# Splitting weights 2048 columns at a time, and moving the tokens' sums, in a float32 two-layer decoder trunk

## The chip, the cores and the metric

The kernel runs on one core of a Trainium2 chip. The metric is the device time of one execution in microseconds (us). Five engines work side by side and meet at semaphores: PE multiplies matrices, DVE and ACT do elementwise work, SP issues the DMAs that bring weights in, POOL is hardly used. Each engine takes its own instructions strictly in the order in which they stand in its queue, except that PE loads weights ahead.

## The reference

All arithmetic is float32. Cut to what matters here:

```python
D_MODEL = 2048; SEQ = 256; DEPTH = 2; N_Q_HEADS = 12; N_KV_HEADS = 4; N_MEM_HEADS = 4; D_FF = 4 * D_MODEL

for layer in range(DEPTH):
    # 12 query heads in 4 groups, each group with one K and V head; layer 0 has sinks and a window
    proj = h @ w_in[layer]                  # q, k, v and the memory heads' queries
    self_out = attention(q, k, v)
    mem_out = memory_attention(qm, mem, w_mem_kv[layer])
    mix = concatenate([self_out, mem_out]) @ w_o[layer]
    h = layer_norm(ALPHA * h + mix, ...)
    ffn = square(relu(h @ w_up[layer])) @ w_down[layer]
    h = layer_norm(ALPHA * h + ffn, ...)
return h
```

## The kernel before

**Products.** PE has no full float32 product at full rate, so every weight and activation is split in two parts, `hi` (a cast on ACT) and `lo` (the rest, a subtraction on DVE): `split`, lines 95 to 97. A product is then three matmuls, hi by hi, lo by hi and hi by lo. Every weight of the model passes through this split once, streamed from memory in tiles of 2048 columns (1 MB) by SP.

**Buffers.** A raw tile sits in one of `NRAW = 4` slots. Its split parts go to buffers `whi` and `wlo` of 1024 columns, `NHI = 7` of each, so a tile needs two of each. A buffer comes free when PE has done its last matmul with it; the cast that fills it next waits for that.

**The program's stages, per layer.** First the projections of the attention: `wform` computes K or Q of one head from one weight tile, 16 steps of k. When its last step is done, `wform_sum` adds the two halves of the result (`sb` on ACT at line 197, then `kt` or `qt` on DVE at line 198). Per group there is one K and three Q. The heads' attention runs in stages hooked into the projections that follow: at step k = 10 of the next projection PE computes a head's scores (lines 343 and 344, from `qt` and `kt`), at k = 14 it transposes an earlier head's weights, at k = 4 it multiplies by V. Then come the memory heads' queries (scores at line 370), the output projection (`aform`), a layer norm (`normed`), and the MLP.

**The MLP.** It works in chunks of 2048 hidden columns, four per layer: two "up" groups (`v_` = 0 and 1), which make the hidden activations, and two "down" groups, which use them. Each is an `mlp_group` of eight weight tiles ("units", K = 256 each) in the order `ORDER`. Units 0 and 1 are "fast": they stand third and fifth and use seven block products in place of eight, with sums of weight blocks (`t`, lines 116 to 120) and sums of activation blocks (`fast_acts`). The sums of the layer's input (`sum_h`) are made once per layer, before its first such group. The sums of a chunk's hidden activations (`sum_g`) are made from `gt[0]`. What an up group has made is transposed in hooks of the group after it (`UHOOKS`: in its first and second unit, lines 426 to 429), and `sum_g` is made in the third of these hooks of the up group with `v_` = 1.

**What sets the order.** The source calls the operations in the order of the loops, and a scheduler that builds the program reorders each engine's queue by its own estimates. So a cast for a later weight tile can stand ahead of a small operation that PE waits for, or behind it.

Of the kernel before, what the change touches and what calls it, by code (L numbers as in the profile page):

```python
# [8 lines left out]
F32 = mybir.dt.float32  # L9
# [6 lines left out]
P = 128  # L16
# [15 lines left out]
SLOPES = [2.0 ** (-8.0 * (i + 1) / HEADS) for i in range(HEADS)]  # L32
FAR = -1e33
NRAW = 4
NHI = 7
NLG = 4
HOLD = 13
HOLDF = 14
# [26 lines left out]
WHOOKS = (10, 14, 4)  # L65
NWARM = 2
FILL = (10, 11, 12, 16)
ORDER = (2, 3, 0, 4, 1, 5, 6, 7)
FAST = (0, 1)
UHOOKS = ((0, 3), (1, 0), (1, 2), (1, 3))  # L70
WTAIL = ((1, 2), (2, 0), (3, 1), (5, 2), (7, 1), (9, 2))

# [2 lines left out]
def trunk(ctx: ExitStack, tc: tile.TileContext, a: dict, out: bass.AP):  # L75
# [23 lines left out]
    def fast_weights(src):  # L99

        raw = wp.tile([P, 2048], F32, name="raw", tag="raw", bufs=NRAW)
        nc.sync.dma_start(raw, src)
        b = raw.rearrange("p (q c) -> p q c", q=4)
        t_ = wp.tile([P, 4, 512], F32, name="t", tag="raw", bufs=NRAW)
        tiles = []

        def pair(s, n):
            hi = wp.tile([P, 1024], F32R, name="whi", tag="whi", bufs=NHI)  # L110
            lo = wp.tile([P, 1024], F32R, name="wlo", tag="wlo", bufs=NHI)
            split(hi[:, :n], lo[:, :n], s)
            tiles.extend([(hi[:, c:c + 512], lo[:, c:c + 512]) for c in range(0, n, 512)])

        pair(raw[:, :1024], 1024)
        nc.vector.tensor_tensor(t_[:, 0:2], b[:, 0:2], b[:, 2:3].broadcast_to([P, 2, 512]), ALU.subtract)
        pair(b[:, 3], 512)
        pair(t_[:, 0:2].rearrange("p q c -> p (q c)"), 1024)
        nc.vector.tensor_tensor(t_[:, 2], b[:, 1], t_[:, 0], ALU.add)
        nc.vector.tensor_tensor(t_[:, 3], b[:, 3], t_[:, 2], ALU.subtract)  # L120
        pair(t_[:, 2:4].rearrange("p q c -> p (q c)"), 1024)
        return dict(zip(("B11", "B22", "B21", "T1", "T3", "T2", "T4"), tiles))

    def fast_acts(x, s_):


        raw = wp.tile([P, 2048], F32, name="x_f", tag="raw", bufs=NRAW)
        f = raw[:, :1024].rearrange("p (k t) -> p k t", k=4)
        nc.vector.tensor_tensor(f, x[:, :, 0].bitcast(F32), x[:, :, 1].bitcast(F32), ALU.add)
        a11, a21 = f[:, 0:4:2, :P], f[:, 0:4:2, P:]  # L130
        a12, a22 = f[:, 1:4:2, :P], f[:, 1:4:2, P:]
        s = raw[:, 1024:].rearrange("p (q u t) -> p q u t", q=4, u=2)
        nc.vector.scalar_tensor_tensor(s[:, 0], a21, -1.0, a22, op0=ALU.mult, op1=ALU.subtract)
        nc.vector.scalar_tensor_tensor(s[:, 1], s[:, 0], -1.0, a11, op0=ALU.mult, op1=ALU.subtract)
        nc.vector.tensor_tensor(s[:, 2], a11, a21, ALU.subtract)
        nc.vector.tensor_tensor(s[:, 3], a12, s[:, 1], ALU.subtract)
        split(s_[:, 0], s_[:, 1], raw[:, 1024:])

    def weights(src, parts=1):


        raw = wp.tile([P, 2048], F32, name="raw", tag="raw", bufs=NRAW)
        n = 2048 // parts
        for c in range(0, 2048, n):
            nc.sync.dma_start(raw[:, c:c + n], src[:, c:c + n])
        halves = []
        n = min(n, 1024)
        for s in range(2):
            hi = wp.tile([P, 1024], F32R, name="whi", tag="whi", bufs=NHI)
            lo = wp.tile([P, 1024], F32R, name="wlo", tag="wlo", bufs=NHI)  # L150
            for c in range(0, 1024, n):
                split(hi[:, c:c + n], lo[:, c:c + n], raw[:, s * 1024 + c:s * 1024 + c + n])
            halves.append((hi, lo))
        return halves

    def new_acts(tag, nm):
        return [ap_.tile([P, 4, 2, T], F32R, name=f"{nm}{j}", tag=f"{tag}{j}") for j in range(KT // 4)]
# [74 lines left out]

        return ps, finish

    def mlp_group(src, xts, sums, hooks, early):

        ps = [ps_mm.tile([P, 512], F32, name="ps_g", tag="mm") for _ in range(4)]
        own = {}  # L240
        seen = {}
        last = {}
        plan = []
        for u in ORDER:
            plan.extend([(u, b) for b in range(4)] if u not in FAST else [(u, i) for i in range(7)])

        fast = ("P1", 0, 1, "P5", "P7", "P6", 2)
        for u in ORDER:
            for i in range(7 if u in FAST else 4):
                last[fast[i] if u in FAST else i] = (u, i)  # L250

        def mm3(bank, x, w, st, en):
            (xh, xl), (hi, lo) = x, w
            nc.tensor.matmul(bank, xh, hi, start=st, stop=False)  # L254
            nc.tensor.matmul(bank, xh, lo, start=False, stop=False)  # L255
            nc.tensor.matmul(bank, xl, hi, start=False, stop=en)  # L256

        def tok(k, t):
            return [xts[k // 4][:, k % 4, s, t * P:(t + 1) * P] for s in range(2)]

        left = len([u for u in ORDER if u in FAST])
        for pos, u in enumerate(ORDER):
            k0, k1 = 2 * u, 2 * u + 1
            if u in FAST:
                for i in range(4):
                    hooks.get((pos, i), nothing)()
                if not own:
                    for nm in ("P1", "P5", "P6", "P7"):
                        own[nm] = ps_at.tile([P, 512], F32, name=nm, tag="at")
                w = fast_weights(src[u])  # L270
                sx = [[sums[:, s, q, u % 2] for s in range(2)] for q in range(4)]
                prods = (("P1", tok(k0, 0), "B11"), (0, tok(k1, 0), "B21"), (1, sx[3], "B22"),
                         ("P5", sx[0], "T1"), ("P7", sx[2], "T3"), ("P6", sx[1], "T2"), (2, tok(k1, 1), "T4"))
                for i, (b, x, wn) in enumerate(prods):
                    mm3(own[b] if b in own else ps[b], x, w[wn], b not in seen, last[b] == (u, i))
                    seen[b] = True
                left -= 1
                if not left:
                    early(own)
                continue  # L280
            (h0, l0), (h1, l1) = weights(src[u])
            w = {"B11": (h0[:, :512], l0[:, :512]), "B22": (h0[:, 512:], l0[:, 512:]),
                 "B12": (h1[:, :512], l1[:, :512]), "B21": (h1[:, 512:], l1[:, 512:])}
            for b in range(4):
                hooks.get((pos, b), nothing)()
                t, n = b // 2, b % 2 + 1
                mm3(ps[b], tok(k0, t), w[f"B1{n}"], b not in seen, False)
                mm3(ps[b], tok(k1, t), w[f"B2{n}"], False, last[b] == (u, b))
                seen[b] = True
        return ps  # L290
# [289 lines left out]
    for l in range(LAYERS):  # L580
# [34 lines left out]
        for c in range(FF // CH):  # L615
            gt = new_acts("og", "gT")
            todo = []
            sum_g = ap_.tile([P, 2, 4, 2, P], F32R, name="sum_g", tag="sum_g")
            for v_ in range(CH // 1024):

                hooks = dict(zip(UHOOKS, todo))
                us = [None] * 4
                if c == 0 and v_ == 0 and not more:
                    for nb in range(2):
                        ps, fin = aform([a["wup_s"][nb, i] for i in range(4)], hT, hold=(16 if nb == 0 else 0))
                        if nb == 0:
                            us[0] = relu2(ps[0])
                            fin()
                            us[2] = relu2(ps[1])
                        else:  # L630
                            us[1], us[3] = relu2(ps[0]), relu2(ps[1])
                else:
                    if sum_h is None:
                        sum_h = ap_.tile([P, 2, 4, 2, P], F32R, name="sum_h", tag="sum_h")
                        fast_acts(hT[0], sum_h)
                    acc = []
                    ps = mlp_group(a["wup"][l, c * (CH // 1024) + v_], hT, sum_h, hooks, sums_up(acc))
                    for b in range(4):
                        nc.vector.tensor_tensor(acc[b], acc[b], ps[b], ALU.add)
                        nc.scalar.activation(acc[b], acc[b], AF.Relu)  # L640
                        nc.scalar.activation(acc[b], acc[b], AF.Square)
                    us = acc

                def back(b, v_=v_, us=us, gt=gt, sum_g=sum_g):
                    transposed(us[b], gt[2 * v_ + b % 2], b // 2, 0)
                    if v_ == 0 and b == 2:
                        fast_acts(gt[0], sum_g)
                todo = [lambda b=b, f=back: f(b) for b in (0, 1, 2, 3)]
            last = c == FF // CH - 1
            if last and more:  # L650
# [1 line left out]
            for v_ in range(D // 1024):  # L652
                if last and v_ == 1:
                    for nb in range(2, 4):
                        ps, fin = aform([a["wdn_s"][l, nb - 2, i] for i in range(4)], gt,
                                        hold=(0 if nb == 2 else 8 if more else HOLDF))
                        if nb == 2:
                            for t in range(NT):
                                residual(h, ps, t, nb, False, st)
                    continue  # L660
                ps = mlp_group(a["wdn"][l, v_, 8 * c:8 * c + 8], gt, sum_g, dict(zip(UHOOKS, todo)),
                               sums_down(h, v_, c == 0))
                todo = []
                for b in range(4):
                    residual(h, {b // 2: ps[b]}, b // 2, 2 * v_ + b % 2, False, st if last else None)
# [63 lines left out]
```

## Time and profile before

| | us |
|---|---|
| median of 3 runs | 2082.78 (2081.52 to 2083.8) |
| profiled execution, own time | 2085.73 |
| its span, first to last instruction | 2083.6 |
| PE busy | 2023.7 (97%) |
| DVE busy | 1540.2 (74%) |
| ACT busy | 1045.6 (50%) |
| mean granted TensorE clock | 0.984 of 2.4 GHz |

The span is what the views measure. The execution's own time is 2.1 us longer, and 2.95 us above the median of the runs. An engine's idle time costs time only where PE, which is busy for nearly all of the span, waits for it.

### The profile page before, as it was taken

The numbers are of one execution on the slowest core, as the hardware profiler recorded it, in microseconds if no ns is written. First come the engines' busy times: TensorE is split into PE (matmuls) and PEld (weight loads), VectorE is DVE, ScalarE is ACT, GpSimd is POOL, SyncE is SP. The second block draws the span as 40 slices with busy tenths as digits, with TensorE's granted clock in tenths as the row PEclk, the third lists the DMA queues.
The fourth block names the chain that finished last, engine by engine and source line by source line (L and its number), as shares of the span: only waits on it lengthen the run. The fifth ranks groups of instructions, "written<-read, shape, count | busy, mean of one in ns | idle before, by whom it ended". The sixth has DMA issues, their size and how long they took to land.

```text
span 2083.6 us, 23980 instructions
## 1 busy us (share of the span) xinstructions
PE 2023.7 (97%) x9326; PEld 1675.4 (80%) x9326; DVE 1540.2 (74%) x1951; ACT 1045.6 (50%) x1351; POOL 1.2 (0%) x8
## 2 busy tenths in 40 slices
PE   9999999999999999999999999999999999999997
PEld 7888888788778878878888888778887887888786
DVE  6566669688597868768885665769786876877785
ACT  5555535554464455456444554346445544654551
POOL 0000000000000000000000000000000000000000
PEclk9999999999999999999999999999999999999999
DMA  9644545455356545445754445425654554564562
GB/s 330 255 143 160 202 162 203 160 204 181 142 208 220 197 157 205 175 146 219 271 222 171 153 162 202 142 103 211 221 194 161 203 177 146 214 219 173 205 220 81
DMA packets 56273, 391.63 MB, mean 188 GB/s; under 512 B 6368, under 2 KB 6368, under 8 KB 9696
## 3 DMA queue, kind: packets, MB, share of 16 engines
q1 hardware_dynamic: 56160, 390.10, 52.1%
q8 instruction: 73, 1.20, 0.2%
q14 instruction: 40, 0.33, 0.0%
HBM read 387.98 MB, written 2.10 MB: 187 GB/s over the span
## 4 chain that ended last, share of the span: by engine, by line
PE 92%; DVE 6%; ACT 1%; issue 0%; DMA 0%; SPq 0%; DVEq 0%; ACTq 0%
PE ps_g L256 17%; PE ps_g L255 17%; PE ps_g L254 17%; PE ps_w L189 7%; PE ps_a L211 5%; PE ps_a L212 5%; PE ps_a L213 5%; PE ps_w L191 4%; PE P L254 3%; PE P L256 3%; PE P L255 3%; PE pt_h L426 2%; PE ps_m L536 1%; PE ps_m L538 1%; PE ps_m L537 1%; DVE h L419 1%
## 5 line engine op out<-in xcount | busy, mean ns | idle before, releaser
L97 DVE TENSOR_TENSOR wlo<-raw,whi 128x1024 fp32r<-128x1024 f32 (+1 forms) x706 | 815.7, 1174 | 329.0 <-ACT whi L96 324.9
L96 ACT CAST whi<-raw 128x1024 fp32r<-128x1024 f32 (+1 forms) x706 | 693.5, 1014 | 596.3 <-PE ps_g L256 323.6
L255 PE MATMUL ps_g<-wlo,hT 128*128 128x512 f32 x780 | 305.8, 392 | 0.1
L256 PE MATMUL ps_g<-whi,hT 128*128 128x512 f32 x780 | 305.9, 392 | 0.0
L254 PE MATMUL ps_g<-whi,hT 128*128 128x512 f32 x780 | 302.6, 395 | 0.9 <-ACT whi L96 0.7
L254 PE MATMUL ps_g<-whi,gT 128*128 128x512 f32 x728 | 285.3, 393 | 0.0
L256 PE MATMUL ps_g<-whi,gT 128*128 128x512 f32 x728 | 283.5, 390 | 0.0
L255 PE MATMUL ps_g<-wlo,gT 128*128 128x512 f32 x728 | 283.4, 390 | 0.0
L96 ACT CAST whi<-t 128x1024 fp32r<-128x1024 f32 x116 | 122.0, 1052 | 120.9 <-PE ps_g L256 45.0
L254 PEld LDWEIGHTS ps_g<-whi,hT 128*128 128x128 f32 x780 | 147.8, 190 | 33.7 <-ACT whi L96 3.8
L255 PEld LDWEIGHTS ps_g<-wlo,hT 128*128 128x128 f32 x780 | 147.7, 189 | 31.3 <-DVE wlo L97 0.5
L256 PEld LDWEIGHTS ps_g<-whi,hT 128*128 128x128 f32 x780 | 147.6, 189 | 31.0
L97 DVE TENSOR_TENSOR wlo<-t,whi 128x1024 fp32r<-128x1024 f32 x116 | 141.6, 1223 | 41.2 <-ACT whi L96 40.9
L256 PEld LDWEIGHTS ps_g<-whi,gT 128*128 128x128 f32 x728 | 136.7, 188 | 28.8
L255 PEld LDWEIGHTS ps_g<-wlo,gT 128*128 128x128 f32 x728 | 136.8, 188 | 27.6
L254 PEld LDWEIGHTS ps_g<-whi,gT 128*128 128x128 f32 x728 | 136.6, 188 | 27.2
L189 PE MATMUL ps_w<-hT,whi 128*128 128x512 f32 x320 | 119.9, 414 | 0.0
L189 PE MATMUL ps_w<-xT,whi 128*128 128x512 f32 x320 | 119.9, 414 | 0.0
L211 PE MATMUL ps_a<-whi,ot 128*128 128x512 f32 x256 | 101.7, 397 | 0.0
L213 PE MATMUL ps_a<-whi,ot 128*128 128x512 f32 x256 | 99.8, 390 | 0.0
L212 PE MATMUL ps_a<-wlo,ot 128*128 128x512 f32 x256 | 99.7, 389 | 0.0
L429 DVE TENSOR_TENSOR gT<-pt_h,gT 128x512 fp32r<-128x512 f32 x64 | 43.9, 688 | 67.0 <-ACT gT L428 67.0
(184 smaller groups left out, 2910.1 us busy)
## 6 DMA issues: line engine op xcount, KB each, us to landing
raw<-in_wup_dram SPq DMA_DIRECT2D x120, 1024.0 KB, 4.9
raw<-in_wdn_dram SPq DMA_DIRECT2D x112, 1024.0 KB, 4.9
raw<-in_wo_dram SPq DMA_DIRECT2D x32, 1024.0 KB, 4.8
raw<-in_wq_dram SPq DMA_DIRECT2D x24, 1024.0 KB, 4.8
raw<-in_wdn_s_dram SPq DMA_DIRECT2D x16, 1024.0 KB, 4.9
raw<-in_wmk_dram SPq DMA_DIRECT2D x8, 1024.0 KB, 6.2
raw<-in_wv_dram SPq DMA_DIRECT2D x8, 1024.0 KB, 7.3
raw<-in_wk_dram SPq DMA_DIRECT2D x8, 1024.0 KB, 4.8
```

The lines of the kernel that those rows point to most:

```text
L96: nc.scalar.copy(hi, src)
L97: nc.vector.tensor_tensor(lo, src, hi.bitcast(F32), ALU.subtract)
L189: nc.tensor.matmul(ps, hi[:, kk:kk + P], x.rearrange("p s t -> p (s t)"), start=(k == 0), stop=False)
L191: nc.tensor.matmul(ps[:, :T], lo[:, kk:kk + P], x[:, 0], start=False, stop=(k == KT - 1))
L211: nc.tensor.matmul(ps[t], xh, hi, start=st, stop=False)
L212: nc.tensor.matmul(ps[t], xh, lo, start=False, stop=False)
L213: nc.tensor.matmul(ps[t], xl, hi, start=False, stop=en)
L254: nc.tensor.matmul(bank, xh, hi, start=st, stop=False)
L255: nc.tensor.matmul(bank, xh, lo, start=False, stop=False)
L256: nc.tensor.matmul(bank, xl, hi, start=False, stop=en)
L426: nc.tensor.transpose(pt[:, k], src[:, k * P:(k + 1) * P], ident)
L429: nc.vector.tensor_tensor(xt[:, :, 1, t * P:(t + 1) * P], pt, hi.bitcast(F32), ALU.subtract)
```

## The change

The split buffers become 2048 columns wide, four of each: 8192 columns in place of 7168. A weight tile is split by one cast and one subtraction. In a fast unit the first 1536 columns (B11, B22, B21) are split at once, then all four sums of weight blocks are made, and all 2048 of their columns are split at once; the order of the blocks in memory is changed so that these 1536 are adjacent. The sums of the tokens (activation blocks) become a generator in two steps: `sum_h` is made in hooks of the first and second unit of the first group that uses it, `sum_g` in hooks at the sixth and seventh unit of the up group with `v_` = 1. Their buffers share tags with `v` and `mk`, and are split 512 columns at a time. `UP` and `DOWN` hold the same order and the same two fast units as before, so PE's products are the same.

```diff
-NHI = 7
+NHI = 4
...
-ORDER = (2, 3, 0, 4, 1, 5, 6, 7)
-FAST = (0, 1)
+UP = ((2, 3, 0, 4, 1, 5, 6, 7), 2)
+DOWN = ((2, 3, 0, 4, 1, 5, 6, 7), 2)
...
-        def pair(s, n):
-            hi = wp.tile([P, 1024], F32R, name="whi", tag="whi", bufs=NHI)
-            lo = wp.tile([P, 1024], F32R, name="wlo", tag="wlo", bufs=NHI)
+        def pairs(s, n):
+            hi = wp.tile([P, 2048], F32R, name="whi", tag="whi", bufs=NHI)
+            lo = wp.tile([P, 2048], F32R, name="wlo", tag="wlo", bufs=NHI)
             split(hi[:, :n], lo[:, :n], s)
...
-        pair(raw[:, :1024], 1024)
-        nc.vector.tensor_tensor(t_[:, 0:2], b[:, 0:2], b[:, 2:3].broadcast_to([P, 2, 512]), ALU.subtract)
-        pair(b[:, 3], 512)
-        pair(t_[:, 0:2].rearrange("p q c -> p (q c)"), 1024)
+        pairs(raw[:, :1536], 1536)
+        nc.vector.tensor_tensor(t_[:, 0:2], b[:, 0:2], b[:, 3:4].broadcast_to([P, 2, 512]), ALU.subtract)
         nc.vector.tensor_tensor(t_[:, 2], b[:, 1], t_[:, 0], ALU.add)
-        nc.vector.tensor_tensor(t_[:, 3], b[:, 3], t_[:, 2], ALU.subtract)
-        pair(t_[:, 2:4].rearrange("p q c -> p (q c)"), 1024)
+        nc.vector.tensor_tensor(t_[:, 3], b[:, 2], t_[:, 2], ALU.subtract)
+        pairs(t_.rearrange("p q c -> p (q c)"), 2048)
...
-    def fast_acts(x, s_):
+    def fast_acts(xs, units):
+        parts = []
+        for j in range(0, len(units), 2):
...
+            parts += [s[:, u] for u in range(n)]
+        yield
+        for (hi, lo), s in zip(units, parts):
+            split(hi, lo, s)
+        yield
...
     def weights(src, parts=1):
-        halves = []
-        n = min(n, 1024)
-        for s in range(2):
-            hi = wp.tile([P, 1024], F32R, name="whi", tag="whi", bufs=NHI)
-            lo = wp.tile([P, 1024], F32R, name="wlo", tag="wlo", bufs=NHI)
-            for c in range(0, 1024, n):
-                split(hi[:, c:c + n], lo[:, c:c + n], raw[:, s * 1024 + c:s * 1024 + c + n])
+        hi = wp.tile([P, 2048], F32R, name="whi", tag="whi", bufs=NHI)
+        lo = wp.tile([P, 2048], F32R, name="wlo", tag="wlo", bufs=NHI)
+        for c in range(0, 2048, n):
+            split(hi[:, c:c + n], lo[:, c:c + n], raw[:, c:c + n])
+        return [(hi[:, c:c + 1024], lo[:, c:c + 1024]) for c in (0, 1024)]
...
-                        sum_h = ap_.tile([P, 2, 4, 2, P], F32R, name="sum_h", tag="sum_h")
-                        fast_acts(hT[0], sum_h)
+                        sum_h = sum_units(UP[1], ("sum_h0", "sum_h1", "pts"))
+                        steps = fast_acts(hT, sum_h)
+                        hooks[0, 0] = hooks[1, 1] = lambda s=steps: next(s)
+                    if v_ == 1:
+                        steps = fast_acts(gt, sum_g)
+                        hooks[5, 0] = hooks[6, 0] = lambda s=steps: next(s)
...
-                    if v_ == 0 and b == 2:
-                        fast_acts(gt[0], sum_g)
```

The first place is ACT's queue in the first up group with `v_` = 1 of layer 0. The names `gT0` and `gT1` are the transposed hidden activations of the group before; `whi_3297` (before) and the casts after it are the first fast unit's weights. Before:

```order
L428 CAST gT1_2850<-pt_h_3237 128x4x128
L428 CAST gT0_2849<-pt_h_3256 128x4x128
L428 CAST gT1_2850<-pt_h_3277 128x4x128
L96 CAST sum_g_2853<-x_f_3263 128x1024
L96 CAST whi_3297<-raw_3294 128x1024
L96 CAST whi_3302<-raw_3294 128x512
L96 CAST whi_3306<-t_3296 128x1024
```

And now, where `whi_3050` holds the first fast unit's sums of weight blocks (its `raw` part is cast further up), `whi_3108` and `whi_3115` are the second fast unit's, and `whi_3151` is the unit's after that:

```order
L97 CAST whi_3050<-t_3042 128x2048
L439 CAST gT0_2647<-pt_h_2972 128x4x128
L97 CAST whi_3077<-raw_3075 128x2048
L439 CAST gT1_2648<-pt_h_2991 128x4x128
L439 CAST gT0_2647<-pt_h_3010 128x4x128
L439 CAST gT1_2648<-pt_h_3023 128x4x128
L97 CAST whi_3108<-raw_3105 128x1536
L97 CAST whi_3115<-t_3107 128x2048
L97 CAST whi_3151<-raw_3149 128x2048
L97 CAST sums_2651<-x_f_3155 128x512
L97 CAST sums_2652<-x_f_3155 128x512
```

All of the first fast unit's casts now stand ahead of the transposes' casts, and the tokens' sums behind those of the second.

The second place is DVE's queue in the attention of layer 0, at the end of a group's last Q projection. `lg`, `mx`, `nm`, `den` and `rec` are an earlier head's softmax; `qt_1309` (before) and `qt_1223` (now) are the query that PE needs for the scores. Before:

```order
L346 SCALAR_TENSOR_TENSOR lg_1344<-dist_a_399,ps_s_1341 128x384
L351 TENSOR_REDUCE mx_1346<-lg_1344 128x1 x2
L354 TENSOR_SCALAR nm_1349<-mx_1346,nsink_411 128x2
L364 TENSOR_TENSOR den_1351<-den_1351,es_1354 128x2
L316 RECIPROCAL rec_1357<-den_1351 128x2
L198 TENSOR_TENSOR qt_1309<-ps_w_1320,sb_1379 128x256
```

And now:

```order
L357 SCALAR_TENSOR_TENSOR lg_1254<-dist_a_373,ps_s_1251 128x384
L362 TENSOR_REDUCE mx_1256<-lg_1254 128x1 x2
L365 TENSOR_SCALAR nm_1259<-mx_1256,nsink_385 128x2
L98 TENSOR_TENSOR wlo_1492<-raw_1489,whi_1491 128x2048
L375 TENSOR_TENSOR den_1261<-den_1261,es_1264 128x2
L212 TENSOR_TENSOR qt_1223<-ps_w_1230,sb_1289 128x256
```

A 2048-column subtraction now stands ahead of `den` and the query.

## Rows read from the trace of the kernel before

**Rows 1.** The page, busy time of each engine, share of the span, instructions

```profile
PE 2023.7 (97%) x9326; PEld 1675.4 (80%) x9326; DVE 1540.2 (74%) x1951; ACT 1045.6 (50%) x1351; POOL 1.2 (0%) x8
```

**Rows 2.** Waits of PE: total us, times, longest

```profile
PE P L254 <- ACT whi L96: 38.3, 16, 3.5
```

**Rows 3.** Windows: stretch, length, busy by engine, granted clock, DMA share, GB/s

```profile
513.42:608.03 94.61, 89.81 (x390) 73.14 (x388) 68.39 (x76) 49.69 (x60) 0.00 (x0) 0.96 0.49 178
608.03:694.24 86.21, 86.21 (x389) 71.41 (x388) 73.49 (x83) 44.31 (x51) 0.00 (x0) 1.00 0.55 196
1388.54:1440.97 52.43, 47.56 (x204) 38.11 (x202) 40.09 (x46) 26.93 (x34) 0.00 (x0) 0.93 0.48 175
```

**Rows 4.** Timeline, ACT and PE, third unit of an up group: start, length, instruction

```profile
389.19 1.04 ACT L96 CAST sum_g<-x_f 128x1024 fp32r<-128x1024 f32 x1 [2.24 <-DVE x_f L136]
390.14 1.56 ACT L96 CAST whi<-raw 128x1024 fp32r<-128x1024 f32 x2
...
391.24 0.50 PE L254 MATMUL P<-whi,hT 128*128 128x512 f32 x1 [3.51 <-ACT whi L96]
...
393.76 0.80 PE L254 MATMUL P<-whi,sum_h 128*128 128x512 f32 x1 [1.27 <-ACT whi L96]
```

**Rows 5.** Timeline, the same place in the down group that follows

```profile
429.68 1.04 ACT L96 CAST whi<-t 128x1024 fp32r<-128x1024 f32 x1
...
439.98 0.39 PE L254 MATMUL P<-whi,gT 128*128 128x512 f32 x1
```

**Rows 6.** Groups by shape, DVE and ACT: busy, mean ns, idle before

```profile
L97 DVE TENSOR_TENSOR wlo<-raw,whi 128x1024 fp32r<-128x1024 f32 x644 | 776.0, 1221 | 326.9 <-ACT whi L96 322.8
L97 DVE TENSOR_TENSOR wlo<-raw,whi 128x512 fp32r<-128x512 f32 x62 | 42.3, 686 | 2.0 <-ACT whi L96 2.0
...
L96 ACT CAST whi<-raw 128x1024 fp32r<-128x1024 f32 x644 | 657.1, 1052 | 552.4 <-PE ps_g L256 282.4 <-PE ps_a L213 156.2 <-PE ps_w L189 63.0
...
L96 ACT CAST whi<-raw 128x512 fp32r<-128x512 f32 x62 | 38.4, 620 | 43.9 <-PE ps_g L256 41.2 <-DMA raw<-in_wmv_dram 2.1
```

**Rows 7.** Timeline of the attention, a group's second Q, then its third

```profile
149.72 1.05 ACT L96 CAST whi<-raw 128x1024 fp32r<-128x1024 f32 x1 [2.44 <-PE ps_w L189]
...
151.95 0.15 DVE L364 TENSOR_TENSOR den<-den,es 128x2 f32<-128x2 f32 x1
...
152.22 0.40 DVE L198 TENSOR_TENSOR qt<-ps_w,sb 128x256 f32<-128x256 f32 x1
...
153.17 0.38 PE L343 MATMUL ps_s<-kt,qt 128*128 128x128 f32 x2
...
155.91 0.39 PE L189 MATMUL ps_w<-xT,whi 128*128 128x512 f32 x1
...
160.46 0.38 PE L343 MATMUL ps_s<-kt,qt 128*128 128x128 f32 x2
```

**Rows 8.** Timeline, the next group's first Q, then a memory head's query

```profile
170.28 1.05 ACT L96 CAST whi<-raw 128x1024 fp32r<-128x1024 f32 x1
...
172.50 0.42 DVE L198 TENSOR_TENSOR qt<-ps_w,sb 128x256 f32<-128x256 f32 x1
...
174.36 0.38 PE L343 MATMUL ps_s<-kt,qt 128*128 128x128 f32 x2
...
213.97 1.05 ACT L96 CAST whi<-raw 128x1024 fp32r<-128x1024 f32 x1
...
217.53 1.02 PE L370 MATMUL ps_m<-mk,qt 128*128 128x256 f32 x4
```

**Rows 9.** Timeline of PE and windows, layer norm of layer 1's attention

```profile
1336.58 1.32 PE L426 MATMUL pt_h<-ident,h 128*128 128x128 f32 x8 [2.04 <-DVE h L420]
...
1351.87 1.29 PE L426 MATMUL pt_h<-ident,h 128*128 128x128 f32 x8 [1.64 <-DVE h L420]
...
1338.10:1341.50 3.40, 3.40 (x11) 2.75 (x11) 3.23 (x6) 1.01 (x2) 0.00 (x0) 0.50 0.60 246
1349.00:1353.00 4.00, 2.33 (x14) 1.53 (x12) 3.86 (x10) 0.47 (x1) 0.00 (x0) 1.00 0.17 70
```

More of the change, by code (lines that the diff above doesn't have):

```diff
@@ L122, in fast_weights @@
+        pairs(t_.rearrange("p q c -> p (q c)"), 2048)
         return dict(zip(("B11", "B22", "B21", "T1", "T3", "T2", "T4"), tiles))
-    def fast_acts(x, s_):
[L127 to L137, printed above, removed]
+    def fast_acts(xs, units):
+        parts = []
+        for j in range(0, len(units), 2):
+            n = len(units[j:j + 2])
+            x = xs[j // 2][:, :2 * n]
+            raw = wp.tile([P, 2, 8, P], F32, name="x_f", tag="raw", bufs=NRAW)
+            f = raw[:, 0, :4 * n].rearrange("p (k t) c -> p k (t c)", t=2)
+            nc.vector.tensor_tensor(f, x[:, :, 0].bitcast(F32), x[:, :, 1].bitcast(F32), ALU.add)
+            a11, a21 = f[:, 0:2 * n:2, :P], f[:, 0:2 * n:2, P:]
+            a12, a22 = f[:, 1:2 * n:2, :P], f[:, 1:2 * n:2, P:]
+            s = raw[:, 1, :4 * n].rearrange("p (u q) c -> p u q c", q=4)
+            nc.vector.scalar_tensor_tensor(s[:, :, 0], a21, -1.0, a22, op0=ALU.mult, op1=ALU.subtract)
+            nc.vector.scalar_tensor_tensor(s[:, :, 1], s[:, :, 0], -1.0, a11, op0=ALU.mult, op1=ALU.subtract)
+            nc.vector.tensor_tensor(s[:, :, 2], a11, a21, ALU.subtract)
+            nc.vector.tensor_tensor(s[:, :, 3], a12, s[:, :, 1], ALU.subtract)
+            parts += [s[:, u] for u in range(n)]
[3 more added lines that the diff above has]
+        yield
@@ L139, in weights, with sum_units @@
+    def sum_units(n, tags):
+        units = []
+        for tag in tags[:n]:
+            if tag == "pts":
+                units.append([ap_.tile([P, 4, P], F32R, name="sums", tag="pts", bufs=2) for _ in range(2)])
+            else:
+                t_ = ap_.tile([P, 2, 4, P], F32R, name="sums", tag=tag)
+                units.append([t_[:, s] for s in range(2)])
+        return units
     def weights(src, parts=1):
@@ L145, in weights @@
             nc.sync.dma_start(raw[:, c:c + n], src[:, c:c + n])
-        halves = []
-        n = min(n, 1024)
-        for s in range(2):
-            hi = wp.tile([P, 1024], F32R, name="whi", tag="whi", bufs=NHI)
-            lo = wp.tile([P, 1024], F32R, name="wlo", tag="wlo", bufs=NHI)
-            for c in range(0, 1024, n):
-                split(hi[:, c:c + n], lo[:, c:c + n], raw[:, s * 1024 + c:s * 1024 + c + n])
-            halves.append((hi, lo))
-        return halves
+        hi = wp.tile([P, 2048], F32R, name="whi", tag="whi", bufs=NHI)
[3 more added lines that the diff above has]
+        return [(hi[:, c:c + 1024], lo[:, c:c + 1024]) for c in (0, 1024)]
     def new_acts(tag, nm):
@@ L233, in aform, with mlp_group @@
         return ps, finish
-    def mlp_group(src, xts, sums, hooks, early):
+    def mlp_group(src, xts, sums, hooks, early, order, nfast):
         ps = [ps_mm.tile([P, 512], F32, name="ps_g", tag="mm") for _ in range(4)]
@@ L242, in mlp_group @@
         last = {}
-        plan = []
-        for u in ORDER:
-            plan.extend([(u, b) for b in range(4)] if u not in FAST else [(u, i) for i in range(7)])
         fast = ("P1", 0, 1, "P5", "P7", "P6", 2)
-        for u in ORDER:
-            for i in range(7 if u in FAST else 4):
-                last[fast[i] if u in FAST else i] = (u, i)
+        for u in order:
+            for i in range(7 if u < nfast else 4):
+                last[fast[i] if u < nfast else i] = (u, i)
         def mm3(bank, x, w, st, en):
@@ L259, in tok @@
             return [xts[k // 4][:, k % 4, s, t * P:(t + 1) * P] for s in range(2)]
-        left = len([u for u in ORDER if u in FAST])
-        for pos, u in enumerate(ORDER):
+        left = nfast
+        for pos, u in enumerate(order):
             k0, k1 = 2 * u, 2 * u + 1
-            if u in FAST:
+            if u < nfast:
                 for i in range(4):
@@ L270, in mlp_group @@
                 w = fast_weights(src[u])
-                sx = [[sums[:, s, q, u % 2] for s in range(2)] for q in range(4)]
+                sx = [[s[:, q] for s in sums[u]] for q in range(4)]
                 prods = (("P1", tok(k0, 0), "B11"), (0, tok(k1, 0), "B21"), (1, sx[3], "B22"),
@@ L282, in mlp_group @@
             w = {"B11": (h0[:, :512], l0[:, :512]), "B22": (h0[:, 512:], l0[:, 512:]),
-                 "B12": (h1[:, :512], l1[:, :512]), "B21": (h1[:, 512:], l1[:, 512:])}
+                 "B21": (h1[:, :512], l1[:, :512]), "B12": (h1[:, 512:], l1[:, 512:])}
             for b in range(4):
@@ L617, in trunk @@
             todo = []
-            sum_g = ap_.tile([P, 2, 4, 2, P], F32R, name="sum_g", tag="sum_g")
+            sum_g = sum_units(DOWN[1], ("v", "mk"))
             for v_ in range(CH // 1024):
@@ L633, in trunk @@
                     if sum_h is None:
-                        sum_h = ap_.tile([P, 2, 4, 2, P], F32R, name="sum_h", tag="sum_h")
-                        fast_acts(hT[0], sum_h)
+                        sum_h = sum_units(UP[1], ("sum_h0", "sum_h1", "pts"))
[4 more added lines that the diff above has]
+                        hooks[5, 0] = hooks[6, 0] = lambda s=steps: next(s)
                     acc = []
-                    ps = mlp_group(a["wup"][l, c * (CH // 1024) + v_], hT, sum_h, hooks, sums_up(acc))
+                    ps = mlp_group(a["wup"][l, c * (CH // 1024) + v_], hT, sum_h, hooks, sums_up(acc), *UP)
                     for b in range(4):
@@ L642, in trunk, with back @@
                     us = acc
-                def back(b, v_=v_, us=us, gt=gt, sum_g=sum_g):
+                def back(b, v_=v_, us=us, gt=gt):
                     transposed(us[b], gt[2 * v_ + b % 2], b // 2, 0)
-                    if v_ == 0 and b == 2:
-                        fast_acts(gt[0], sum_g)
                 todo = [lambda b=b, f=back: f(b) for b in (0, 1, 2, 3)]
@@ L661, in trunk @@
                 ps = mlp_group(a["wdn"][l, v_, 8 * c:8 * c + 8], gt, sum_g, dict(zip(UHOOKS, todo)),
-                               sums_down(h, v_, c == 0))
+                               sums_down(h, v_, c == 0), *DOWN)
                 todo = []
@@ L696, in quads @@
         b = w.reshape(k // 256, 2, P, n // 1024, 2, 512).transpose(3, 0, 2, 1, 4, 5)
-        return np.ascontiguousarray(np.stack([b[:, :, :, 0, 0], b[:, :, :, 1, 1], b[:, :, :, 0, 1], b[:, :, :, 1, 0]],
+        return np.ascontiguousarray(np.stack([b[:, :, :, 0, 0], b[:, :, :, 1, 1], b[:, :, :, 1, 0], b[:, :, :, 0, 1]],
                                              axis=3)).reshape(n // 1024, k // 256, P, 2048)
```

## The prediction

> **What bounds the kernel now.** I read the engines' busy times first: PE is busy for 97% of the span, DVE for 74%, ACT for 50% [rows 1]. So PE sets the time, and only what makes PE wait, or lowers its clock, can be won or lost. PE's matmuls are the same in number and kind in both kernels.
>
> Next I read the waits of PE. One line carries nearly all: 38.3 us in 16 waits of the first fast product for its weights' cast on ACT [rows 2]. The windows place them. A pair of up groups and a pair of down groups have the same work on PE (388 weight loads each), yet the up pair takes 94.61 us and the down pair 86.21, and the granted clock is 0.96 in the one and 1.00 in the other [rows 3]. The timeline of one such place shows the cause: ACT must cast `sum_g`, which waits for DVE's sums, before it casts the weights of the first fast unit. PE idles for 3.51 us and again for 1.27 us, and its matmuls then run at half rate for a while (a step of 0.43 us where 0.23 is usual), so the clock has fallen to the lower of its two levels, 1.2 GHz [rows 4]. In the down group the hooks transpose in the same way, but nothing of `sum_g` is made, and the sums of weights have been cast 10 us before PE's first fast product begins, without a wait [rows 5].
>
> **The change part by part.**
>
> *The tokens' sums move.* In the new order ACT casts all of the first fast unit's weights before the transposes' casts, as the down group does now, and `sum_g` after those of the second fast unit. Each up group with `v_` = 1 then costs what its PE work costs. There are eight: seven stand in whole pairs, each worth 94.61 - 86.21 = 8.4 us; the eighth, in layer 1's first chunk, stands alone and takes 52.43 us [rows 3], against half of a down pair with one more set of transposes, 43.1 + 0.7 = 43.8 us, so 8.6 us. Together 7 x 8.4 + 8.6 = 67.4 us. The half-clock stretch is inside this, since the windows contain it. What is late next in these groups? DVE has 68.4 us of work in an up pair [rows 3]; in 86.2 us that leaves it 17.8 us idle. I went through the first three units with these durations. The first fast product's weights are split before the group begins, the sums of weight blocks about 8 us into it, and PE needs them about 14 us into it. The sums of the tokens, 4 us on DVE, fall beside the fifth and sixth unit, whose weights have a lead of some 6 us; they are needed only in the next group. So I cost the moved step at nothing; if that cover were gone, it would cost its length, 4 us a place.
>
> *Wider splits.* A cast of 1024 columns takes 1.05 us and of 512 columns 0.62, so by a straight line 2048 take 1.05 + 2 x 0.43 = 1.92 us. A subtraction takes 1.22 and 0.69 us, so 2048 take 2.29 us [rows 6]. The work is the same. One tile now costs one instruction where it cost two, but neither engine is the bound, so what is saved per instruction is worth nothing.
>
> What the width costs is delay for whoever stands behind it. In the attention a query reaches PE by a short chain after its projection's end: `sb` on ACT, `qt` on DVE, then the scores on PE, ten steps into the next projection. In the new order a 2048-column cast, which waits for the buffer that this same projection's end frees, stands ahead of `sb`; and its 2048-column subtraction stands ahead of `qt`. Before, each was half as long, or stood behind. Behind the subtraction wait `den`, the query, and with the query PE itself. For the group's second Q: the buffer is free and the cast starts at 149.72, and `qt` is done at 149.72 + 1.92 + 2.29 + 0.15 (`den`) + 0.40 = 154.48; PE wants it at 153.17 [rows 7]. That is a wait of 1.3 us. For the third Q the last matmul with the buffer ends at 155.91 + 0.39 = 156.30, the query is ready at 156.30 + 4.76 = 161.06, and PE wants it at 160.46: 0.6 us [rows 7]. For the first Q no `den` stands there: 170.28 + 4.61 = 174.89 against 174.36, so 0.5 us [rows 8]. K is needed later than one projection, and waits for nothing. Per group of four projections that is 2.4 us, in eight groups 19.2 us. Among the memory heads three queries stand behind such a subtraction; the one I worked out is ready at 213.97 + 4.76 = 218.73 and wanted at 217.53 [rows 8], so 1.2 us, and three make 3.6 us. The attention loses about 22.8 us.
>
> No row shows these waits, so I bound them. Below: nothing, if the casts start earlier than the buffers let me think. Above: all 27 of them at the full lengthening of both instructions, 0.87 + 1.07 = 1.94 us, without the slack that the rows show: 52 us. I take 22.8, since it comes from the very places.
>
> The Trainium skill has a rule that speaks against this part ("Perfetto Trace Analysis", "Optimizing Scalar/DVE Operations"): where ScalarE and VectorE are not saturated but cause bubbles elsewhere, break instructions up. By that rule the attention pays, as I reckon it does. The same section prices a grouped instruction at some 60 ns saved on VectorE and 93 ns on ScalarE; by that alone the sum would have the attention's 22.8 us at nothing. The busy shares above are those of engines that are not saturated, so the first half of the rule is the one that applies.
>
> *The rest.* The layer norms, the start and the output projections get the same work in other pieces. The first group of layer 0 now has its first tile split before the norm ends; the norm in layer 1 has a residual moved ahead of PE's transposes, but one more quarter of a tile to hide behind. I cost these at nothing together, with 4 us to each side, the size of the two waits of 2.04 and 1.64 us that stand in layer 1's norm [rows 9].
>
> *Sum.* The profiled execution took 2085.73 us, with a span of 2083.6. 2085.73 - 67.4 + 22.8 = 2041.1 us. It stands 2.95 us above the median of the runs shown, 2082.78, so I predict a median of 2038 us.
>
> **The rivals.**
>
> *The attention doesn't wait.* For it: PE has no wait anywhere in the attention now, and four tiles of lead are more than three and a half. Against it: the buffer that the cast waits for is freed by the projection's own end, so lead doesn't help. It would give 2082.78 - 67.4 = 2015 us.
>
> *PE still waits in the MLP.* The first fast unit's sums are now split as one piece, only after all four are made, and its buffer comes free only when the group before has ended. If half of the 67.4 us stayed, the time would be 2038 + 34 = 2072 us. Against it: the 6 us of lead that I count above, and the down groups, which run free with nearly that order.
>
> *The short waits lower the clock (slower than before).* After a wait of 2.04 us, with light transposes, PE's clock stood at 0.50 for 3.4 us; after one of 1.64 us it stayed at 1.00 [rows 9]. If the new waits in the attention, 0.5 to 1.3 us each, had the effect of the longer one, each of the 27 would cost 3.4 x 0.5 = 1.7 us more, 46 us in all: 2038 + 46 = 2084, level with before. If they had the effect of those in the MLP, where the rate stays low for about 6.8 us, it would be 27 x 3.4 = 92 us: 2130 us. The change is slower from the point at which these waits cost more than 67.4 us, 2.5 us each.
>
> The Trainium skill ("TensorE: Matmul & The Clock Gate", Part 1) says that the throttled state is the default and that activity releases it; by it many small gaps could cool PE. The trace agrees for a long gap and not for the 1.64 us one.
>
> **How the numbers follow.** The forecast 0.62, no wait in the attention 0.18, half of the MLP's waits staying 0.10, the clock 0.06, something that I do not see, either way, 0.04. For 8 in 10: the forecast's own bounds are 2085.73 - 2.95 - 67.4 = 2015 with no wait in the attention and 2067 with all 52 us, or 4 us beyond with the norms. I take 2012 to 2062, which holds the first rival and most of the forecast's upper half, and leaves out the other two. Two kernels of this length can be told apart from about 0.2%, 4 us. Faster: the forecast, the first two rivals and half of the unseen, 0.92, less a little for a bad mixture, 0.90. Slower: half of the clock's and of the unseen, 0.06. The same: 0.04.
>
> **What would show it.** In the profile after: PE's waits for `whi` in the first fast product gone, up pairs and down pairs within 1 us of each other and a clock of 1.00 in both. In the attention, new waits of PE at the scores for `qt`, three in each four projections, of about 1.3, 0.6 and 0.5 us. The forecast is wrong if up pairs still take over 90 us, if the scores wait for nothing, or if the clock falls in the attention.

## The result, and the profile after

The changed kernel takes a median of 2019.42 us (2017.79 to 2019.5), against 2082.6 us before on the same chip: a ratio of 0.9695, 95% interval 0.9678 to 0.9711. I had forecast 2038 us, in a range of 2012 to 2062. The direction was right and the time lies in the range, but the gain is 63 us where I forecast 45. One term of the sum was wrong by 20 us.

The busy times of the engines, from the page of the changed kernel:

```profile
PE 1996.1 (99%) x9326; PEld 1659.4 (82%) x9326; DVE 1505.6 (75%) x1554; ACT 992.7 (49%) x954; POOL 1.2 (0%) x8
```

PE runs the same 9326 matmuls as before [rows 1] and is now busy for 99% of a span of 2016.0 us. The waits of PE are what is left of its idle time:

```profile
PE pt_h L437 <- DVE h L431: 3.2, 1, 3.2
PE ps_m L547 <- ACT whi L97: 1.7, 2, 1.5
PE ps_warm L94 <- DVE warm L91: 1.5, 1, 1.5
...
```

The line of the first fast product, 38.3 us in 16 waits [rows 2], is gone, and no other line of that size has come. The windows of the same three stretches as in [rows 3] (length, busy of PE, PEld, DVE, ACT, POOL, granted clock, DMA share, GB/s):

```profile
504.19:590.45 86.26, 86.26 (x390) 71.41 (x389) 69.90 (x61) 47.27 (x40) 0.00 (x0) 1.00 0.55 195
590.45:676.66 86.21, 86.21 (x390) 71.42 (x388) 68.74 (x59) 42.07 (x31) 0.00 (x0) 1.00 0.54 195
1354.55:1398.61 44.06, 44.06 (x204) 36.50 (x203) 37.52 (x37) 24.59 (x23) 0.00 (x0) 1.00 0.53 191
```

A pair of up groups now takes 86.26 us at a clock of 1.00, like a pair of down groups. It took 94.61 at 0.96. The place of [rows 4] in the timelines of ACT and PE:

```profile
376.40 1.90 ACT L97 CAST whi<-t 128x2048 fp32r<-128x2048 f32 x1
378.61 0.59 ACT L439 CAST gT<-pt_h 128x512 fp32r<-128x512 f32 x1 [0.31 <-PE pt_h L437]
...
386.65 0.39 PE L265 MATMUL P<-whi,hT 128*128 128x512 f32 x1
```

The sums of weight blocks are cast at 376.40, ahead of the transposes' casts and 10 us before PE's first fast product. It starts without a wait, as in the down group of [rows 5].

In the attention the picture is less plain. This is the second Q of [rows 7], in the timelines of ACT, DVE, PE and PE's weight loads (PEld):

```profile
148.05 1.91 ACT L97 CAST whi<-raw 128x2048 fp32r<-128x2048 f32 x1 [4.51 <-PE ps_w L203]
...
150.00 2.29 DVE L98 TENSOR_TENSOR wlo<-raw,whi 128x2048 fp32r<-128x2048 f32 x1 [1.87 <-ACT whi L97]
152.20 0.15 DVE L375 TENSOR_TENSOR den<-den,es 128x2 f32<-128x2 f32 x1
152.28 0.42 DVE L212 TENSOR_TENSOR qt<-ps_w,sb 128x256 f32<-128x256 f32 x1
...
151.44 0.39 PE L203 MATMUL ps_w<-xT,whi 128*128 128x512 f32 x1
151.67 0.28 PE L205 MATMUL ps_w<-xT,wlo 128*128 128x256 f32 x1
151.78 0.39 PE L203 MATMUL ps_w<-xT,whi 128*128 128x512 f32 x1
...
152.81 0.30 PEld L354 LDWEIGHTS ps_s<-kt,qt 128*128 128x128 f32 x2 [0.26 <-issue]
...
152.84 0.46 PE L354 MATMUL ps_s<-kt,qt 128*128 128x128 f32 x2
```

The query comes as late as I reckoned: the cast waits for the end of the query's own projection, and `qt` is done 152.70 - 148.05 = 4.65 us after the cast's start, where I had 4.76. At the scores' former place PE would have come to them at 151.44, where step k = 10 of the next projection begins, 1.26 us before the query was done. But PE's weight load waits only 0.26 us, not 1.3, because the scores have moved on PE. In the kernel before they stood between the steps k = 9 and k = 10:

```
L191 MATMUL ps_w_1320<-xT2_415,wlo_1317 128x256
L343 MATMUL ps_s_1341<-kt_1101,qt_1237 128x128
L344 MATMUL ps_s_1341<-kt_1101,qt_1237 128x256
L189 MATMUL ps_w_1320<-xT2_415,whi_1316 128x512
```

and in the changed kernel they stand seven matmuls later, inside step k = 13:

```
L203 MATMUL ps_w_1230<-xT3_390,whi_1226 128x512
L354 MATMUL ps_s_1251<-kt_1027,qt_1155 128x128
L355 MATMUL ps_s_1251<-kt_1027,qt_1155 128x256
L205 MATMUL ps_w_1230<-xT3_390,wlo_1227 128x256
```

For the group's third and first Q the scores stand three matmuls later (for the first Q of a layer's first group, seven). The waits that remain show in the waits of PE's weight loads, with no releaser named ("issue"):

```profile
PEld ps_s L354 <- issue: 4.8, 22, 0.3
```

Since both kernels run the same count of matmuls, the start of the k-th in one profile can be set against the k-th in the other (the moved scores blur this by a fraction of a microsecond). The differences by stage:

| stage | forecast, us | measured, us |
|---|---|---|
| MLP, both layers | -67.4 | -67.3 (eight places of 8.3 to 8.5, and small change) |
| attention, both layers | +22.8 | +3.0 |
| start | 0 | -2.4 |
| norms and the groups beside them | 0 | -0.9 |
| span | -44.6 | -67.6 |

By the medians of runs the gain is 63.2 us; the profiled execution of before stood 2.95 us above its median, and that of the changed kernel 1.6 us below its own.

### The profile page after: what moved, and what is told of

It is laid out like the page before. It is cut to its first block, busy times and chain, and to the rows that moved or that the text cites. A ratio compares the mean times of both kernels' runs of the same rounds, so it can differ in the third digit from the quotient of the medians.

```text
span 2016.0 us, 22875 instructions
## 1 busy us (share of the span) xinstructions
PE 1996.1 (99%) x9326; PEld 1659.4 (82%) x9326; DVE 1505.6 (75%) x1554; ACT 992.7 (49%) x954; POOL 1.2 (0%) x8
## 4 chain that ended last, share of the span: by engine, by line
PE 96%; DVE 2%; ACT 1%; issue 0%; DMA 0%; SPq 0%; DVEq 0%; ACTq 0%
PE ps_g L265 17%; PE ps_g L267 17%; PE ps_g L266 17%; PE ps_w L203 7%; PE ps_a L225 6%; PE ps_a L226 5%; PE ps_a L227 5%; PE ps_w L205 4%; PE P L267 3%; PE P L266 3%; PE P L265 3%; PE pt_h L437 2%; PE ps_m L548 1%; PE ps_m L549 1%; PE ps_m L547 1%; DVE wlo L98 1%
## 5 line engine op out<-in xcount | busy, mean ns | idle before, releaser
L98 DVE TENSOR_TENSOR wlo<-raw,whi 128x2048 fp32r<-128x2048 f32 (+2 forms) x357 | 775.5, 2173 | 380.3 <-ACT whi L97 379.1
L97 ACT CAST whi<-raw 128x2048 fp32r<-128x2048 f32 (+2 forms) x357 | 649.5, 1820 | 670.6 <-PE ps_g L267 408.9
L265 PEld LDWEIGHTS ps_g<-whi,gT 128*128 128x128 f32 x728 | 136.7, 188 | 27.3
L97 ACT CAST whi<-t 128x2048 fp32r<-128x2048 f32 x58 | 110.8, 1911 | 93.9 <-DVE t L119 75.2
L98 DVE TENSOR_TENSOR wlo<-t,whi 128x2048 fp32r<-128x2048 f32 x58 | 133.0, 2292 | 25.1 <-ACT whi L97 23.9
L205 PE MATMUL ps_w<-hT,wlo 128*128 128x256 f32 x320 | 92.0, 288 | 0.0
```

The source lines that it names most:

```text
L97: nc.scalar.copy(hi, src)
L98: nc.vector.tensor_tensor(lo, src, hi.bitcast(F32), ALU.subtract)
L205: nc.tensor.matmul(ps[:, :T], lo[:, kk:kk + P], x[:, 0], start=False, stop=(k == KT - 1))
```

## The experiments

My theory was now this. The MLP's gain comes from the place of `sum_g` alone, and the width gives nothing. The attention lost little because the scheduler, which knows that the wider splits are longer, placed the scores later. The rivals: the wide buffers bring the gain; the queries were never late; short waits would cost clock.

**Late sums alone.** The kernel before, with one edit:

```diff
-                    if v_ == 0 and b == 2:
-                        fast_acts(gt[0], sum_g)
+                    if v_ == 1:
+                        hooks[5, 0] = lambda g=gt, s=sum_g: fast_acts(g[0], s)
```

> The kernel before with one edit: sum_g is made in the hook at the sixth unit of the up group with v_ = 1, in one piece; splits stay 1024 columns wide, seven buffers. Theory (what cost the time was the place of the cast of sum_g ahead of the first fast unit's casts): PE's 16 waits of 38.3 us go, up pairs take 86.2 us in place of 94.6, and with eight places at 8.3 us the time falls by 66.7 us to about 2016 us, a ratio of 0.968; nothing is lost in the attention. Rival (the wide buffers or the new order inside a fast unit were needed too): half or more of the waits stay, 2050 us or more.

Measured: 2015.52 us, ratio 0.9673 (0.9658 to 0.9687). Its waits of PE:

```profile
PE pt_h L426 <- DVE h L420: 4.2, 2, 2.2
PE ps_m L536 <- ACT whi L96: 1.6, 1, 1.6
PE ps_warm L93 <- DVE warm L90: 1.5, 1, 1.5
PE ps_g L254 <- ACT whi L96: 0.7, 1, 0.7
```

Four lines of code bring the whole gain. The time is 4 us below that of the full change, about the least that can be told apart. The eight places give 8.3 to 8.5 us each here too.

**Wide buffers alone.** The changed kernel, with `sum_g` back in the third transposing hook:

```diff
-                    if v_ == 1:
-                        steps = fast_acts(gt, sum_g)
-                        hooks[5, 0] = hooks[6, 0] = lambda s=steps: next(s)
...
+                    if v_ == 0 and b == 2:
+                        for _ in fast_acts(gt, sum_g):
+                            pass
```

> The changed kernel with sum_g made and split again in the third transposing hook of the up group with v_ = 1; all buffers stay 2048 wide. Theory (the place of the sums is the whole gain): ACT casts all four transposes and sum_g before either cast of the first fast unit, so PE waits there at least as long as in the kernel before, some 5 us in each of eight groups, and its clock falls: 2019 + 67 = 2086 us, between 2075 and 2100. Rival (the wider splits bring the gain): within 5 us of 2019 us.

Measured: 2097.9 us, ratio 1.0069 (1.0054 to 1.0084): 0.7% slower than before. ACT and PE in the timeline of the same place:

```profile
389.13 1.14 ACT L97 CAST sums<-x_f 128x512 fp32r<-128x512 f32 x2 [2.24 <-DVE x_f L140]
390.17 1.47 ACT L97 CAST whi<-raw 128x1536 fp32r<-128x1536 f32 x1
...
391.69 0.52 PE L265 MATMUL P<-whi,hT 128*128 128x512 f32 x1 [4.03 <-ACT whi L97]
...
394.65 0.79 PE L266 MATMUL P<-wlo,hT 128*128 128x512 f32 x1 [1.59 <-DVE wlo L98]
```

The wait of [rows 4] is back and longer, 4.03 and 1.59 us in place of 3.51 and 1.27, since the cast behind the sums is now 1536 columns wide and the subtraction too. The up pair takes 96.30 us at a clock of 0.96:

```profile
514.79:611.09 96.30, 89.52 (x390) 72.27 (x388) 67.42 (x57) 47.85 (x40) 0.00 (x0) 0.96 0.48 174
```

So the width, with the new order inside a fast unit that comes with it, makes a wait behind a late cast worse. The move brings everything.

**Scores pinned, scores free.** To see what the queries' lateness costs when PE's order does not give way, I fixed the attention's order: each projection's weight tile four ahead is split before `sb` and `qt`, and PE may not start the tenth step of the next projection before the scores. The second run has the first edit without the second. Shortened:

```diff
 def wform_sum:
+        if queue:
+            ahead.append(weights(queue.pop(0)))
+        with tc.issue_after(cut[0].ins):
             nc.scalar.copy(sb, ps[:, T:])
+        with tc.issue_after(cut[1].ins):
             nc.vector.tensor_tensor(dst, ps[:, :T], sb, ALU.add)
 def wform:                              # only in the pinned run
+            with tc.issue_after(pin[-1].ins):
                 nc.tensor.matmul(ps, hi[:, kk:kk + P], ...)
```

`cut` holds the last tile's cast and subtraction, `pin` the last scores.

> The changed kernel with the attention's order fixed by hand: the 2048-column cast ahead of sb and the 2048-column subtraction ahead of qt for every projection, and the scores on PE ahead of the tenth step of the next projection, where the kernel before had them. Theory (the queries are as late as I reckoned, and the waits did not come since the scores stand 3 to 7 matmuls later on PE): PE waits at the scores about 0.5, 1.3 and 0.6 us in each group of four projections and 1 to 2 us for memory heads, 20 us in all where the changed kernel lost 3: 2039 us, between 2032 and 2048, at a clock of 1.00. Rival A (the queries come sooner than I reckoned): under 2025 us. Rival B (short waits lower the clock): over 2060 us, with stretches of the attention at a granted clock of 0.50.

> The same order of casts and subtractions by hand as in the run with pinned scores, but the scores stand where the scheduler puts them, which is the changed kernel's place, 3 to 7 matmuls later than before. Theory: waits of 0.2 to 0.3 us at the scores, 2019 to 2023 us. If the order by hand itself costs something, it shows here: over 2028 us, and the run with pinned scores is then to be read against this one.

Measured: 2047.0 us with the scores pinned, ratio 0.9828 (0.9811 to 0.9844), and 2019.35 us with them free, ratio 0.9691 (0.9676 to 0.9705). The place of the scores alone is worth 27.7 us. From the pinned run, the waits of PE, three scores of a group in its timeline, and a window of the attention in layer 0:

```profile
PE ps_s L365 <- DVE qt L223: 25.5, 24, 1.8
```

```profile
153.94 0.46 PE L365 MATMUL ps_s<-kt,qt 128*128 128x128 f32 x2 [0.47 <-DVE qt L223]
...
162.15 0.46 PE L365 MATMUL ps_s<-kt,qt 128*128 128x128 f32 x2 [1.76 <-DVE qt L223]
...
170.73 0.46 PE L365 MATMUL ps_s<-kt,qt 128*128 128x128 f32 x2 [1.08 <-DVE qt L223]
```

```profile
92.00:212.00 120.00, 107.18 (x618) 92.36 (x616) 71.07 (x139) 53.27 (x113) 0.00 (x0) 1.00 0.38 132
```

These are the 24 waits of my forecast: 0.5, 1.8 and 1.1 us in layer 0 where I had 0.5, 1.3 and 0.6; in layer 1 they are 0.5, 1.5 and 0.8, and the first Q of each layer waits 1.0 to 1.1. So the queries are late, which refutes rival A, and in the profiled execution the clock stays at 1.00 through all 24 waits, which with the time refutes rival B. What kept the waits away is the scheduler's place for the scores. The waits come to 25.5 us where I had 19.2, and so the theory's 2039 us is 8 us below the time, which lies within the window that I gave. Most of the excess belongs to this run and not to the changed kernel: with the scores pinned, ACT's softmax of the head before stands ahead of the cast, which for the second Q starts 0.64 us after the buffer's last matmul (157.45 against 156.81), where in the changed kernel it started 0.04 us after. The memory heads' scores were not pinned, so this run does not test what I gave them; their loads wait 0.6 us in all.

**Halves in the wide buffers.** The changed kernel, but a weight tile is split in two instructions:

```diff
 def weights:
+        n = min(n, 1024)
         for c in range(0, 2048, n):
             split(hi[:, c:c + n], lo[:, c:c + n], raw[:, c:c + n])
```

> The changed kernel, but a weight tile outside the fast units is split 1024 columns at a time into its 2048-column buffer. Theory (the attention's 3 us are the longer cast and subtraction ahead of sb and qt): the queries are ready earlier, the scheduler puts the scores back to their former place on PE, the 22 short waits of 4.8 us at the scores go, and the time is 2016 to 2017 us, a ratio of 0.968. Rival (the buffer, freed as a whole by the projection's end, is what delays): waits at the scores stay and the time is 2019 us, 0.9695.

Measured: 2014.17 us (2013.29 to 2014.38), ratio 0.967 (0.9657 to 0.9684). It is the lowest median of all, 5.2 us below the changed kernel, though not to be told from the late sums alone (ratio 0.9673), and no wait at the scores is listed. The second Q in its timelines of ACT, DVE and PE:

```profile
147.96 0.35 ACT L212 COPY sb<-ps_w 128x256 f32<-128x256 f32 x1
...
148.22 2.00 ACT L97 CAST whi<-raw 128x1024 fp32r<-128x1024 f32 x2
...
148.37 0.40 DVE L213 TENSOR_TENSOR qt<-ps_w,sb 128x256 f32<-128x256 f32 x1
...
149.29 2.36 DVE L98 TENSOR_TENSOR wlo<-raw,whi 128x1024 fp32r<-128x1024 f32 x2
...
150.83 0.38 PE L355 MATMUL ps_s<-kt,qt 128*128 128x128 f32 x2
```

The scores are back at the tenth step, and the query is ready 2 us before them. The buffer is still freed as a whole, which refutes the rival. With the shorter instructions the scheduler puts both casts behind `sb` and both subtractions behind `qt`. So the attention's loss goes away when a tile is split in two, but by way of the new order; what two shorter instructions ahead of `sb` and `qt` would cost, this run does not show. Between the two profiles the spans differ by 4.0 us, and matched matmuls put 3.0 of these in the attention and 1.0 beside layer 0's norm. The two casts take 2.00 us together, against 1.91 for the wide one, and the two subtractions 2.36 against 2.29: so little did the width save.

**Sums between the fast units.** As with late sums alone, but two units earlier:

```diff
-                        hooks[5, 0] = lambda g=gt, s=sum_g: fast_acts(g[0], s)
+                        hooks[3, 0] = lambda g=gt, s=sum_g: fast_acts(g[0], s)
```

> As the run with the late sums only, but sum_g is made in the hook of the fourth unit, between the two fast units: its cast stands ahead of the second fast unit's casts. Theory (a sum's cast costs only where the fast unit behind it has no lead left): the second fast unit starts some 19 us into the group, its weights are ahead by several us, PE waits nothing or under 1 us a place: 2015 to 2023 us. Rival (any fast unit behind the sums waits): about 4.8 us of waits and 3.4 us of half clock in each of eight places, near 2080 us.

Measured: 2016.3 us, ratio 0.9681 (0.9667 to 0.9694), not to be told from the late sums. ACT's timeline, and PE at the second fast unit's first product:

```profile
388.35 1.05 ACT L96 CAST sum_g<-x_f 128x1024 fp32r<-128x1024 f32 x1 [2.21 <-DVE x_f L136]
389.31 1.56 ACT L96 CAST whi<-raw 128x1024 fp32r<-128x1024 f32 x2
...
395.78 0.39 PE L254 MATMUL P<-whi,hT 128*128 128x512 f32 x1
```

The cast of `sum_g` waits for DVE's sums as it did in [rows 4], and the second fast unit's casts wait behind it as the first's did then. But PE takes the first of them at 395.78, 4.9 us after the casts end, and no wait of PE in the MLP comes from it. Here a cast that blocks ACT for 3 us costs nothing, since the weights are ahead by more than that.

**A longer hold.** The largest wait left stands in layer 1's norm. As with late sums alone:

```diff
-HOLD = 13
+HOLD = 16
```

> As the run with the late sums only, with HOLD 16 in place of 13: in the layer norm of layer 1's attention three more steps of the second token half are held back, 3 x 3 matmuls of 0.23 us, to stand between the first half's last matmul and the transposes that wait for DVE. Theory (the two waits of PE there, 4.2 us, are DVE's chain, which then starts 2 us earlier against PE): 2 us less, 2013.5 us. Rival (the wait moves to the second half): no change, 2015.5 us.

Measured: 2015.55 us, ratio 0.9677 (0.9663 to 0.9691): no change. The two waits of 2.03 and 2.19 us have become one:

```profile
1302.75 3.36 PE L426 MATMUL pt_h<-ident,h 128*128 128x128 f32 x16 [3.49 <-DVE h L420]
```

My theory failed here: the work held back does not cover the chain on DVE, and the scheduler put 16 transposes in one run behind the wait. How much of the wait the longer hold itself took away, this run can't show.

## Why the prediction was right, and where it was wrong

*The tokens' sums: right in mechanism and size.* I forecast 67.4 us and the MLP gave 67.3. A whole up pair gained 8.35 us for a forecast 8.4, the single one 8.37 for 8.6. That the half-clock stretch is inside the difference of windows was the useful choice: in PE's waits alone one sees only 38.3 us. The rest is nearly all clock. In the kernel before, the clock is at 0.50 for 6.83 us behind each of the eight places, here the one of [rows 4]:

```profile
392.61:399.44 6.83, 5.68 (x13) 4.46 (x14) 5.68 (x8) 3.62 (x4) 0.00 (x0) 0.50 0.38 143
```

Eight such stretches cost 8 x 6.83 x 0.5 = 27.3 us, which with the 38.3 us makes 65.6. The cover that I counted held, also with the sums two units earlier.

*Wider splits, the work: right.* 1.91 us for a cast (forecast 1.92) and 2.29 for a subtraction (forecast 2.29). That neither engine's saving is worth time was right too: DVE lost 34.6 us of busy time and ACT 52.9, and the version with halves is still faster.

*Wider splits, the attention: the failed step.* I forecast 22.8 us and it was 3.0. The step that failed is "PE wants it at 153.17": I took the moment at which PE asks for a query from a row of before, and said only that the matmuls are the same in number and kind. Their order is not the same. The scheduler had moved the scores three matmuls later for the first and third Q and seven for the second. By the rows above a matmul with `whi` takes PE 0.23 us and one with `wlo` 0.11, so that is some 0.6 and 1.3 us: all of the 0.5, 1.3 and 0.6 us that I had. What is left at the loads is 0.2 to 0.3 us each, and by the signs that I named this part failed: no wait of 1.3, 0.6 and 0.5 us stands in the profile. Pinned to their former place, the scores wait 25.5 us, a third more than I said.

*The first rival* ("the attention doesn't wait", 2015 us) came nearest to the time, but not for the reason that I gave it, tiles of lead: the cast still starts at the end of the query's own projection. That the time lies in my range was partly luck: I had drawn the range down to 2012 so that it holds this rival, while my own sum was 19 us too high.

*The Trainium skill* ("Perfetto Trace Analysis", "Optimizing Scalar/DVE Operations") advises to break up instructions of engines that are not saturated where they cause bubbles elsewhere. The run with halves agrees: 5.2 us faster. The overheads of an instruction that it states for operands in SBUF, some 93 ns on ScalarE and 60 ns on VectorE, agree with the rows as well: 2.00 - 1.91 = 0.09 us and 2.36 - 2.29 = 0.07 us.

*PE still waits in the MLP* (2072 us) did not happen: no wait of the first fast product is left. *The clock* (2084 us or more) did not fall in the attention, neither with the short waits of the changed kernel nor with the 24 longer ones of the pinned run.

*The rest*, costed at nothing with 4 us to each side, gave 3.3 us, 2.4 of them at the start, where PE's wait for the first weights was shorter. This needs no change: the run with late sums alone has the instructions of the kernel before at its start, and had 2.3 us of it too. Its first weight tile landed at 6.18 us where that of the profile of before landed at 7.37, and its clock rose at 10.3 us in place of 13.7. So the start differs from one execution to the next, and that part of the gain is most likely not the change's. The two waits in layer 1's norm became one of 3.2 us.

## What to carry to other kernels

When an in-order engine casts for several consumers, put the cast that nobody needs soon behind the one with no lead; here that single move was worth 67 us, 38 of them waits and nearly all of the rest a lowered clock. Do not split wider for the sake of fewer instructions where a short chain, such as `sb` and `qt`, passes through the same queues: 0.09 and 0.07 us are saved, and whoever stands behind waits for the whole; here the attention lost 3 us by it, and 25.5 us of waits where PE's order could not give way. And where a scheduler builds the queues, look up in the new order on both sides of a wait, the one that is late and the one that waits, before pricing it by a row of the old trace.

## What the runs showed of the hardware that I had not expected

A wait does not lower TensorE's clock by its length alone. In the kernel before, a wait of 2.04 us in layer 1's norm was followed by a stretch at 0.50, the lower of the two levels, 1.2 GHz [rows 9]. In the run with late sums alone the same two waits, 2.03 and 2.19 us, were followed by none. Its timeline of PE and its windows:

```profile
1300.71 1.32 PE L426 MATMUL pt_h<-ident,h 128*128 128x128 f32 x8 [2.03 <-DVE h L420]
...
1314.99 1.29 PE L426 MATMUL pt_h<-ident,h 128*128 128x128 f32 x8 [2.19 <-DVE h L420]
```

```profile
1300.00:1315.00 15.00, 12.08 (x59) 9.49 (x59) 14.82 (x29) 2.35 (x4) 0.00 (x0) 1.00 0.49 182
1315.00:1320.00 5.00, 4.94 (x27) 3.72 (x28) 4.28 (x7) 3.30 (x5) 0.00 (x0) 1.00 0.00 0
```

In the run with the sums between the fast units, a wait of 2.04 us at the first of these two places was followed by a stretch at 0.50 again:

```profile
1300.96 1.97 PE L426 MATMUL pt_h<-ident,h 128*128 128x128 f32 x8 [2.04 <-DVE h L420]
...
1300.96:1304.37 3.41, 3.41 (x14) 3.01 (x15) 2.74 (x5) 1.17 (x2) 0.00 (x0) 0.50 0.99 394
```

After the wait of 3.2 us in the changed kernel the clock was at 0.50 too:

```profile
1305.94:1309.35 3.41, 3.41 (x10) 2.83 (x11) 3.05 (x6) 1.05 (x2) 0.00 (x0) 0.50 0.21 82
```

What decides between two waits of 2 us was not settled.
